# A decoder block on one core: the mLSTM norm taken for two heads at a time, its heads finished later, and the projection behind it begun later

## The chip, the cores and the metric

The program runs on one core of one Trainium2 chip. The metric is the device time of one execution in microseconds (us), from the first to the last instruction with what lies around it; lower is better. Five engines work from instruction streams of their own: TensorE (PE, with its weight loads as PEld), VectorE (DVE), ScalarE (ACT), GpSimd (POOL) and SyncE (SP), which here only issues transfers. Each stream is worked off in its order; an instruction that waits for a semaphore holds up all that stand behind it in the same stream.

## The reference, cut to what matters

One layer of a decoder with 2048 tokens of width 1024: a combined input projection, eight attention heads and four mLSTM heads side by side, an output projection over both, cross-attention to a small memory, a mixture of experts, and a final norm. The change lies in the mLSTM heads, at the step that turns numerators into normed, gated outputs:

```
num = einsum('bhcls,bhcse->bhcle', s, v) + inter_w * einsum('bhcld,bhcde->bhcle', q, C_prev)
den = sum(s) + inter_w * einsum('bhcld,bhcd->bhcl', q, n_prev)
h   = num / maximum(abs(den), exp(-m_t))
hn  = h * rsqrt(mean(h*h) + EPS)                      # per token and head
y_m = sigmoid(mo) * (hn * g_mhn + skip_m * c)
y   = concatenate([y_att, y_m]) @ w_out
```

Since the norm follows the division, the kernel never divides: it takes `num * rsqrt(mean(num*num) + EPS * max(|den|, exp(-m_t))^2)`.

## The kernel before, in words

The kernel goes through four stages: input projection, heads, cross-attention, experts. Only the heads stage is touched. There three generators are interleaved by priorities:

- `attention` works off eight attention heads, one after the other. Each multiplies scores (tiles sA, sB, L438 and L439), adds a mask and takes the row extreme on DVE (L446), exponentiates on ACT (L447), transposes (tA, tB), splits into a high and a low part on ACT and DVE (L452, L453) and multiplies with the values (oA, oB).
- `mlstm` has 16 steps: for each of four blocks of 512 tokens (`c4`) the four mLSTM heads (`h`). One step loads its tiles over SP's queue (qT, kT, nb, iwb, v), prepares nb and iwb on POOL (L748, L749), multiplies into `po`, carries the state C through DVE (L779) and copies numerators with their denominators into `num` (L781). Behind the copy `finish` of the step before is written: POOL squares num into `sq` (L712), DVE works on small tiles `sm` of 128x4 (L713 to L717, with L716 the sum of squares, and the ten instructions of the helper `rsqrt`, L28 to L32), POOL scales num into `sq` (L719), PE transposes (`ph`, L722), DVE adds the skip part (L723), POOL gates (L724) and SP stores `ym` (L725). Its inputs c2 and mo are loaded at the end of the step.
- `out_m` is the mLSTM part of the output projection, in two halves of the output rows. Each half has 16 steps of 24 matmuls into `pm` (L825 to L827), on columns of `ym` that `mlstm` has stored. POOL and ACT split `ym` first (tiles yml, ymh).

`heads` gives each generator's next step a priority that lies at a fraction of an attention head: mLSTM step i at `MEND * i / 16` heads, a step of the first half of `out_m` between `OSTART` and `OMID`, the second half between `OMID` and `OEND`. A scheduler then writes out one fixed order for each engine. A loop over `done` makes sure that the mLSTM steps that a projection step reads are placed ahead of it.

Of the kernel before, what the change touches and what calls it, by code (L numbers as in the profile page):

```python
# [8 lines left out]
F32 = mybir.dt.float32  # L9
# [3 lines left out]
OP = mybir.AluOpType  # L13
PSUM = bass.MemoryType.PSUM
DRAM = bass.MemoryType.DRAM
P = 128
# [353 lines left out]
def attention(tc, ctx, I, Z, K, marks):  # L370
# [101 lines left out]
    for pair in range(4):  # L472
# [99 lines left out]

        rb = sp.tile([32, 2, P], F32, name=f"rowB{pair}", tag="rowA", bufs=1)
        nc.vector.tensor_copy(rb, by_rows(f"stB{pair}", st[1]))
        w = op.tile([32, 2, P], F32, name=f"w{pair}", tag="w", bufs=1)

        nc.vector.tensor_sub(w[:, 0], rb[:, 0], ra[:, 0])
        nc.vector.tensor_sub(w[:, 1], ra[:, 0], rb[:, 0])
# [110 lines left out]
def mlstm(tc, ctx, I, Z, K, pb):  # L689

    nc = tc.nc

    lp = pool(tc, ctx, "p3l", 2)
    hp = pool(tc, ctx, "p3h", 2)
    cp = pool(tc, ctx, "p3c", 1)

    def const(name, shape):
        t = cp.tile(shape, F32, name="c_" + name)
        nc.sync.dma_start(t, I[name])
        return t  # L700

    yield
    ident, maskM = K["ident"], const("maskM", [P, P])
    decb, colt = K["decb"], K["colt"]
    gh = const("g_mhn", [P, 4])
    nc.vector.tensor_scalar(gh, gh, 0.5, None, op0=OP.mult)

    def finish(h, u, q0, num, c2, mo, hs, ts):

        sq = hp.tile([P, 4, P], F32, name="sq" + u, tag="sq", bufs=1)  # L710
        sm = hp.tile([P, 4, 4], F32, name="sm" + u, tag="sm", bufs=2)
        nc.gpsimd.tensor_mul(sq, num[:, :, 0:P], num[:, :, 0:P])  # L712
        nc.vector.scalar_tensor_tensor(sm[:, 1], num[:, :, 128], -1.0, num[:, :, 128], op0=OP.mult, op1=OP.max)  # L713
        nc.vector.tensor_tensor(sm[:, 1], sm[:, 1], colt[:, 2, q0:q0 + 4], op=OP.max)
        nc.vector.scalar_tensor_tensor(sm[:, 1], sm[:, 1], EPS, sm[:, 1], op0=OP.mult, op1=OP.mult)
        nc.vector.tensor_reduce(sm[:, 0], sq, axis=mybir.AxisListType.X, op=OP.add)  # L716
        nc.vector.scalar_tensor_tensor(sm[:, 0], sm[:, 0], 1.0 / P, sm[:, 1], op0=OP.mult, op1=OP.add)  # L717
        rsqrt(nc, sm[:, 3], sm[:, 0], sm[:, 1])
        nc.gpsimd.tensor_tensor(sq, num[:, :, 0:P], sm[:, 3].unsqueeze(2).to_broadcast([P, 4, P]), op=OP.mult)  # L719
        ph = pb.tile([P, 4, P], F32, name="ph" + u, tag="b")  # L720
        for i in range(4):
            nc.tensor.transpose(ph[:, i], sq[:, i], ident)  # L722
        nc.vector.scalar_tensor_tensor(c2, ph.rearrange("p i l -> p (i l)"), gh[:, h:h + 1], c2, op0=OP.mult, op1=OP.add)  # L723
        nc.gpsimd.tensor_mul(mo, mo, c2)  # L724
        nc.sync.dma_start(Z["ym"][hs, ts], mo)  # L725

    tail = None
    state = [None] * 4
    for c4 in range(4):
        for h in range(4):  # L730
            if c4 or h:
                yield
            C = state[h]
            u = f"{h}_{c4}"
            hs, ts, q0 = slice(h * P, h * P + P), slice(c4 * 512, c4 * 512 + 512), h * 16 + c4 * 4

            def load(name, src, pool=lp, bufs=2):
                t = pool.tile([P, 512], F32, name=name + u, tag=name, bufs=bufs)
                nc.sync.dma_start(t, src)
                return t  # L740

            qT, kT = (load("qk"[x] + "T", Z["mqk"][x, hs, ts]) for x in range(2))
            nb, iwb = (load(n, Z["gr"][x, q0:q0 + 4, :].rearrange("c l -> (c l)").unsqueeze(0).to_broadcast([P, 512])) for x, n in enumerate(("nb", "iwb")))
            v = lp.tile([P, 4, 129], F32, name="v" + u, tag="v")
            nc.vector.memset(v[:, :, 128:129], 1.0)
            nc.sync.dma_start(v[:, :, 0:P], Z["mv"][ts, h * P:(h + 1) * P].rearrange("(c p) e -> p c e", p=P))
            nb = nb.rearrange("p (c l) -> p c l", l=P)
            nc.gpsimd.tensor_tensor(nb, maskM.unsqueeze(1).to_broadcast([P, 4, P]), nb, op=OP.subtract)  # L748
            nc.gpsimd.tensor_mul(iwb, qT, iwb)  # L749

            pst = pb.tile([P, 4, P], F32, name="pst" + u, tag="b")
            dw = nb
            for i in range(4):
                ws = slice(i * P, i * P + P)
                nc.tensor.matmul(pst[:, i], kT[:, ws], qT[:, ws], start=True, stop=True)
                nc.scalar.activation(dw[:, i], nb[:, i], AF.Exp, bias=colt[:, 0, q0 + i:q0 + i + 1])
            nc.vector.tensor_mul(dw, pst, dw)
            pk = pb.tile([P, 4, P], F32, name="pk" + u, tag="b")
            kw = kT.rearrange("p (i d) -> p i d", i=4)
            for i in range(4):  # L760
                nc.tensor.transpose(pk[:, i], kT[:, i * P:i * P + P], ident)
            nc.vector.tensor_tensor(kw, pk, colt[:, 1, q0:q0 + 4].unsqueeze(2).to_broadcast([P, 4, P]), op=OP.mult)
            num = hp.tile([P, 4, 129], F32, name="num" + u, tag="num", bufs=2)
            for i2 in range(2):
                pt = pb.tile([P, 3, 129], F32, name=f"po{u}{i2}", tag="b")
                po, pl = pt[:, 0:2], pt[:, 2]
                for x in range(2):
                    i = 2 * i2 + x
                    ws = slice(i * P, i * P + P)
                    nc.tensor.matmul(po[:, x], dw[:, i], v[:, i], start=True, stop=(C is None), skip_group_check=True)  # L770
                    if C is not None:
                        nc.tensor.matmul(po[:, x], iwb[:, ws], C, start=False, stop=True, skip_group_check=True)
                    if c4 * 4 + i < 15:
                        nc.tensor.matmul(pl, kw[:, i], v[:, i], start=True, stop=True, skip_group_check=True)
                        Cn = hp.tile([P, 129], F32, name=f"C{u}{i}", tag=f"C{h}", bufs=2)
                        if C is None:
                            nc.vector.tensor_copy(Cn, pl)
                        else:
                            nc.vector.scalar_tensor_tensor(Cn, C, decb[:, q0 + i:q0 + i + 1], pl, op0=OP.mult, op1=OP.add)  # L779
                        C = Cn  # L780
                nc.scalar.copy(num[:, 2 * i2:2 * i2 + 2], po)  # L781
            state[h] = C
            late, tail = tail, lambda h=h, u=u, q0=q0, num=num, hs=hs, ts=ts: finish(h, u, q0, num, c2, mo, hs, ts)
            if late:
                late()

            c2, mo = (load(n, Z[n][hs, ts], hp, 1) for n in ("c2", "mo"))
    tail()


def out_m(tc, ctx, I, Z, pb, half, bufs):
# [40 lines left out]
def heads(tc, I, Z, K):  # L832

    marks = []
    with ExitStack() as ctx:
# [9 lines left out]
        with ExitStack() as c2:  # L845
# [5 lines left out]
            done = 0  # L851
            for t, which, i in sorted(at):

                while which and done < min(16, i // 4 * 4 + 5):
                    go(t, m)
                    done += 1
                if which or i == done:
# [10 lines left out]
WARM = 9  # L868
NS, NT, NO, NB = 2, 2, 2, 2
NPA, NPB = 3, 2  # L870
MEND, OSTART, OMID, OEND = 5.5, 2, 7.3, 7.9


def mm3(nc, out, wh, wl, xh, xl, first, last):
# [996 lines left out]
```

## Time and profile before

| what | value |
|---|---|
| time, median of 3 runs | 2208.98 us (2201.88 to 2212.25) |
| profiled execution: its own time, its span | 2215.31 us, 2213.5 us |
| busy over the span: PE, PEld, DVE, ACT, POOL | 2041.5, 1875.2, 1373.3, 1043.4, 635.0 us |
| heads stage, 588 to 1100 us: PE, PEld, DVE, ACT, POOL busy | 441.89, 413.08, 382.78, 324.35, 225.21 of 512.00 us |
| granted TensorE clock: span, heads stage | 0.958, 0.95 of full speed |

The profiled execution lies 6 us above the median of the three runs. "Busy" is time in which an engine works on an instruction; time in which a DVE instruction is held after it has begun counts as busy too. A busy PE is a modelled figure: matmuls overlap, so their mean durations don't add up to time. The eight attention heads begin at about 589, 658, 718, 772, 838, 891, 957 and 1022 us (the first sA matmul of each), and the stage's last matmuls (`wt`) end at about 1112 us.

### The profile page before, as it was taken

The page shows a single profiled execution, that of the slowest core. Times are in us where ns is not written, and L with a number is a line of the kernel's source. Part 1 is how long each engine was busy: PE and PEld are TensorE (multiplying, and loading weights), DVE is VectorE, ACT ScalarE, POOL GpSimd, SP SyncE. Part 2 cuts the span into 40 slices and gives each one's busy share as a digit, 9 for nine tenths or more (in the row PEclk, how much of TensorE's full clock was granted, in tenths as well). Part 3 has the DMA queues.
Part 4 walks back from the last instruction along what each step waited for, and adds up shares of the span by engine and source line. Part 5 has one row for each costly group of instructions (what it writes and reads, how often), then busy time and mean ns, then how long its engine had stood idle before and what let it go on. Part 6 is the DMA issues. An engine that isn't in the chain of part 4 may idle for free. (4 is left out here: it accounts for less than half of the span.)

```text
span 2213.5 us, 36146 instructions
## 1 busy us (share of the span) xinstructions
PE 2041.5 (92%) x13247; PEld 1875.2 (85%) x13247; DVE 1373.3 (62%) x3315; ACT 1043.4 (47%) x2216; POOL 635.0 (29%) x415
## 2 busy tenths in 40 slices
PE   8999999999888888889969999858999999999996
PEld 6898988988677888879968999857999998889985
DVE  8125741255278889865688788865666565445576
ACT  5223432233266766665534545425555554444462
POOL 3541235421344454543240020142111111121003
PEclk9999999999899999999979999968999999999998
DMA  7544645342697897786552222257878786666596
GB/s 205 178 154 142 215 144 155 113 131 111 174 236 195 242 234 216 208 228 182 180 175 72 100 96 87 87 156 239 247 222 251 202 240 193 168 188 179 152 337 236
DMA packets 276244, 402.45 MB, mean 182 GB/s; under 512 B 28176, under 2 KB 204624, under 8 KB 276016
## 3 DMA queue, kind: packets, MB, share of 16 engines
q1 hardware_dynamic: 262528, 355.11, 52.3%
q0 software_dynamic: 13536, 45.00, 8.3%
q8 instruction: 106, 1.74, 0.3%
q14 instruction: 74, 0.61, 0.1%
HBM read 286.33 MB, written 114.00 MB: 181 GB/s over the span
## 5 line engine op out<-in xcount | busy, mean ns | idle before, releaser
L39 POOL TENSOR_TENSOR wl<-wr,wh 128x1024 fp32r<-128x1024 f32 (+1 forms) x46 | 118.9, 2606 | 256.0 <-ACT wh L38 244.0
L1654 POOL DMA_INDIRECT z_acc<-y,ix x34 | 55.9, 1645 | 407.2 <-DVE y L1646 175.5
L876 PE MATMUL pa<-xl,ww_0h 128*128 128x256 f32 (+5 forms) x512 | 153.0, 307 | 2.2 <-DVE xl L42 2.2
L875 PE MATMUL pa<-xh,ww_1h 128*128 128x256 f32 (+5 forms) x512 | 152.0, 297 | 0.0
L877 PE MATMUL pa<-xh,ww_1l 128*128 128x256 f32 (+5 forms) x512 | 151.7, 296 | 0.0
L876 PE MATMUL pa<-xl,ww_1h 128*128 128x256 f32 (+5 forms) x512 | 151.6, 296 | 0.0
L877 PE MATMUL pa<-xh,ww_0l 128*128 128x256 f32 (+5 forms) x512 | 147.6, 299 | 0.0
L335 PE MATMUL pn<-wl,xh 128*128 128x256 f32 (+1 forms) x512 | 144.9, 283 | 0.0
L334 PE MATMUL pn<-wh,xh 128*128 128x256 f32 (+1 forms) x512 | 144.9, 283 | 0.0
L336 PE MATMUL pn<-wh,xl 128*128 128x256 f32 (+1 forms) x512 | 144.9, 283 | 0.0
L42 DVE SCALAR_TENSOR_TENSOR xl<-pt,f_gf,xh 128x256 fp32r<-128x256 f32 (+5 forms) x128 | 64.3, 515 | 116.5 <-ACT xh L41 116.1
L875 PE MATMUL pa<-xh,ww_0h 128*128 128x256 f32 (+5 forms) x512 | 135.4, 301 | 0.6 <-ACT xh L41 0.6
L41 ACT ACTIVATE xh<-pt,f_gf 128x256 fp32r<-128x256 f32 (+5 forms) x128 | 61.9, 499 | 135.6 <-PE pt L1576 135.2
L38 ACT CAST wh<-wr 128x1024 fp32r<-128x1024 f32 (+3 forms) x49 | 48.4, 1030 | 130.5 <-PE pn L336 58.0
L39 DVE TENSOR_TENSOR ww_1l<-ww_1r,ww_1h 128x512 fp32r<-128x512 f32 x124 | 77.6, 676 | 46.3 <-ACT ww_1h L38 46.2
L876 PEld LDWEIGHTS pa<-xl,ww_0h 128*128 128x128 f32 x512 | 97.8, 192 | 4.8 <-DVE xl L42 2.4
L877 PEld LDWEIGHTS pa<-xh,ww_0l 128*128 128x128 f32 x512 | 97.6, 192 | 0.9
L335 PEld LDWEIGHTS pn<-wl,xh 128*128 128x128 f32 x512 | 97.1, 190 | 0.9
L334 PEld LDWEIGHTS pn<-wh,xh 128*128 128x128 f32 x512 | 97.1, 190 | 0.9
L336 PEld LDWEIGHTS pn<-wh,xl 128*128 128x128 f32 x512 | 96.9, 189 | 0.5
L875 PEld LDWEIGHTS pa<-xh,ww_1h 128*128 128x128 f32 x512 | 97.4, 190 | 0.0
L877 PEld LDWEIGHTS pa<-xh,ww_1l 128*128 128x128 f32 x512 | 97.2, 190 | 0.0
(708 smaller groups left out, 7140.3 us busy)
## 6 DMA issues: line engine op xcount, KB each, us to landing
ww_1r<-w SPq DMA_DIRECT2D x31, 1024.0 KB
ww_0r<-w SPq DMA_DIRECT2D x30, 1024.0 KB
wr<-w_in SPq DMA_DIRECT2D x43, 512.0 KB
w_0r<-w SPq DMA_DIRECT2D x16, 1024.0 KB
w_1r<-w SPq DMA_DIRECT2D x16, 1024.0 KB
z_v<-v SPq DMA_DIRECT2D x32, 256.0 KB
z_mqk<-mq SPq DMA_DIRECT2D x16, 512.0 KB
kk<-z_qkh SPq DMA_DIRECT2D x32, 256.0 KB
```

The source lines that it names most:

```text
L38: a = nc.scalar.copy(hi, src)
L39: b = eng.tensor_sub(lo, src, hi.bitcast(F32))
L41: a = nc.scalar.activation(hi, src, AF.Copy, scale=scale)
L42: b = eng.scalar_tensor_tensor(lo, src, scale, hi.bitcast(F32), op0=OP.mult, op1=OP.subtract)
L334: nc.tensor.matmul(ps[:, :n], xhw, wh[:, k, :], start=(k == 0), stop=False)
L335: nc.tensor.matmul(ps[:, :n], xhw, wl[:, k, :], start=False, stop=False)
L336: nc.tensor.matmul(ps[:, :n], xlw, wh[:, k, :], start=False, stop=(k == KT - 1))
L875: nc.tensor.matmul(out, wh, xh, start=first, stop=False, skip_group_check=True)
L876: nc.tensor.matmul(out, wh, xl, start=False, stop=False, skip_group_check=True)
L877: nc.tensor.matmul(out, wl, xh, start=False, stop=last, skip_group_check=True)
L1654: d = nc.gpsimd.indirect_dma_start(out=Z["acc"], out_offset=bass.IndirectOffsetOnAxis(ap=self.ix[:r, n:n + 1], axis=0), in_=y[:r], in_offs ...
```

## The change

`finish` is cut in two. `norms` takes two heads at once, from one tile `nums` that holds the numerators of both: the squares and their sum are still formed per head, and all other small DVE instructions run once on 128x8 instead of twice on 128x4. `finish` keeps the scaling, the transposes, the gate and the store. Two heads' norms are taken in the odd step; the heads are finished one in each of the next steps, the even one in the first of them. c2 and mo are loaded (`fetch`) behind the finish of the head ahead of them. To make room, iwb has one buffer in place of two, and a small attention tile `w` shares a buffer with wtB. The loop over `done` asks for one mLSTM step more, and `OSTART` goes from 2 to 2.4.

```diff
-        w = op.tile([32, 2, P], F32, name=f"w{pair}", tag="w", bufs=1)
+        w = op.tile([P, 4, P], F32, name=f"w{pair}", tag="wtB")[0:32, 0:2]
...
-    def finish(h, u, q0, num, c2, mo, hs, ts):
-
-        sq = hp.tile([P, 4, P], F32, name="sq" + u, tag="sq", bufs=1)
-        sm = hp.tile([P, 4, 4], F32, name="sm" + u, tag="sm", bufs=2)
-        nc.gpsimd.tensor_mul(sq, num[:, :, 0:P], num[:, :, 0:P])
-        nc.vector.scalar_tensor_tensor(sm[:, 1], num[:, :, 128], -1.0, num[:, :, 128], op0=OP.mult, op1=OP.max)
-        nc.vector.tensor_tensor(sm[:, 1], sm[:, 1], colt[:, 2, q0:q0 + 4], op=OP.max)
+    def norms(c4, h, nums):
+
+        u = f"{h}_{c4}"
+        sm = hp.tile([P, 4, 2, 4], F32, name="sm" + u, tag="sm", bufs=2)
+        em = colt[:, 2, h * 16:h * 16 + 32].rearrange("p (g c) -> p g c", g=2)[:, :, c4 * 4:c4 * 4 + 4]
+        den = nums[:, :, :, 128]
+        nc.vector.scalar_tensor_tensor(sm[:, 1], den, -1.0, den, op0=OP.mult, op1=OP.max)
+        nc.vector.tensor_tensor(sm[:, 1], sm[:, 1], em, op=OP.max)
         nc.vector.scalar_tensor_tensor(sm[:, 1], sm[:, 1], EPS, sm[:, 1], op0=OP.mult, op1=OP.mult)
-        nc.vector.tensor_reduce(sm[:, 0], sq, axis=mybir.AxisListType.X, op=OP.add)
+        for g in range(2):
+            sq = hp.tile([P, 4, P], F32, name=f"sq{u}{g}", tag="sq", bufs=1)
+            nc.gpsimd.tensor_mul(sq, nums[:, g, :, 0:P], nums[:, g, :, 0:P])
+            nc.vector.tensor_reduce(sm[:, 0, g], sq, axis=mybir.AxisListType.X, op=OP.add)
         nc.vector.scalar_tensor_tensor(sm[:, 0], sm[:, 0], 1.0 / P, sm[:, 1], op0=OP.mult, op1=OP.add)
         rsqrt(nc, sm[:, 3], sm[:, 0], sm[:, 1])
-        nc.gpsimd.tensor_tensor(sq, num[:, :, 0:P], sm[:, 3].unsqueeze(2).to_broadcast([P, 4, P]), op=OP.mult)
+        return sm[:, 3]
+
+    def finish(h, u, num, rn, hs, ts):
+        c2, mo = ahead.pop()
+        sq = hp.tile([P, 4, P], F32, name="sn" + u, tag="sq", bufs=1)
+        nc.gpsimd.tensor_tensor(sq, num[:, :, 0:P], rn.unsqueeze(2).to_broadcast([P, 4, P]), op=OP.mult)
...
+    def fetch():
+
+        if tail and not ahead:
+            h, u, _, _, hs, ts = tail[0]
+            ahead.append([load(n + u, n, Z[n][hs, ts], hp, 1) for n in ("c2", "mo")])
...
-            nb, iwb = (load(n, Z["gr"][x, q0:q0 + 4, :].rearrange("c l -> (c l)").unsqueeze(0).to_broadcast([P, 512])) for x, n in enumerate(("nb", "iwb")))
+            nb, iwb = (load(n + u, n, Z["gr"][x, q0:q0 + 4, :].rearrange("c l -> (c l)").unsqueeze(0).to_broadcast([P, 512]), lp, 2 - x) for x, n in enumerate(("nb", "iwb")))
...
-            num = hp.tile([P, 4, 129], F32, name="num" + u, tag="num", bufs=2)
+            if h % 2 == 0:
+                nums = hp.tile([P, 2, 4, 129], F32, name="num" + u, tag="num", bufs=2)
+            num = nums[:, h % 2]
...
-            late, tail = tail, lambda h=h, u=u, q0=q0, num=num, hs=hs, ts=ts: finish(h, u, q0, num, c2, mo, hs, ts)
-            if late:
-                late()
-
-            c2, mo = (load(n, Z[n][hs, ts], hp, 1) for n in ("c2", "mo"))
-    tail()
+
+            if tail:
+                finish(*tail.pop(0))
+            if h % 2:
+                rn = norms(c4, h - 1, nums)
+                for g in range(2):
+                    hg = h - 1 + g
+                    tail.append((hg, f"{hg}_{c4}", nums[:, g], rn[:, g], slice(hg * P, hg * P + P), ts))
+            fetch()
+    while tail:
+        finish(*tail.pop(0))
+        fetch()
...
-                while which and done < min(16, i // 4 * 4 + 5):
+                while which and done < min(16, i // 4 * 4 + 6):
...
-MEND, OSTART, OMID, OEND = 5.5, 2, 7.3, 7.9
+MEND, OSTART, OMID, OEND = 5.5, 2.4, 7.3, 7.9
```

What the scheduler makes of it is seen in the order of each engine's instructions. On DVE before, in the second attention head (the `sm` tiles of mLSTM heads 0 and 1 of block 1), the small `sm` instructions of two heads run through each other, between the attention's mask instructions (L446, shown as ISA) and splits (L453):

```order
L713 SCALAR_TENSOR_TENSOR sm_1_9284<-num_1_9115 128x4
L446 ISA pB_20_5643,stB_4867<-sB_20_5638,b_maskB 128x128
L446 ISA stB_4867 128x1
L32 SCALAR_TENSOR_TENSOR sm_1_9141<-sm_1_9141 128x4
L453 TENSOR_TENSOR ptbl_4863<-tB_0_3_5563,ptbh_4862 128x512
L714 TENSOR_TENSOR sm_1_9284<-sm_1_9284,colt 128x4
L30 SCALAR_TENSOR_TENSOR sm_1_9141<-sm_1_9141 128x4
L446 ISA pB_21_5646,stB_4867<-sB_20_5638,b_maskB 128x256
L446 ISA stB_4867 128x1
L715 SCALAR_TENSOR_TENSOR sm_1_9284<-sm_1_9284 128x4
L31 TENSOR_TENSOR sm_1_9141<-sm_1_9141 128x4
L32 SCALAR_TENSOR_TENSOR sm_1_9141<-sm_1_9141 128x4
```

On DVE after, where the third attention head begins, the same two mLSTM heads have one chain (128x8), with other instructions between its links as before:

```order
L32 SCALAR_TENSOR_TENSOR sm_1_9107<-sm_1_9107 128x8
L797 SCALAR_TENSOR_TENSOR C_11_9171<-C_10_9166,decb,po_10_9162 128x129
L453 TENSOR_TENSOR ptbl_4865<-tB_3_3_5728,ptbh_4864 128x512
L30 SCALAR_TENSOR_TENSOR sm_1_9107<-sm_1_9107 128x8
L446 ISA pA_3_5854,stA_5805<-sA_2_5846,b_maskA 128x256
L446 ISA stA_5805 128x1
L582 TENSOR_TENSOR rowX_5525<-w_5753,rowX_5525 32x128
L583 TENSOR_TENSOR rowB_5748<-w_5753,rowB_5748 32x128
L446 ISA pA_4_5869,stA_5805<-sA_4_5864,b_maskA 128x256
L446 ISA stA_5805 128x1
L31 TENSOR_TENSOR sm_1_9107<-sm_1_9107 128x8
```

DVE's stream has 2906 rows after and 3020 before. On SP's queue in the first attention head before, the loads of mLSTM step 1 (its iwb here) and step 2 stood ahead of the loads of the values vA and vB:

```order
L325 DMA z_mo<-g_3_4788 128x1024
L739 DMA iwb_0_8755<-z_gr 128x512
L746 DMA v_0_8757<-z_mv 128x4x128
L405 DMA kk_5298<-z_qkh 64x1024 x2
L739 DMA qT_0_8833<-z_mqk 128x512
L402 DMA qs_5297<-z_qkh 64x1024
L403 DMA qs_5297<-z_qkl 64x1024
L405 DMA kk_5298<-z_qkh 64x1024 x2
L483 DMA vA_4870<-z_v 32x16x128 x4
L485 DMA vB_4871<-z_v 128x4x128 x4
```

On SP's queue after, iwb of step 1 stands behind them, since its single buffer is free only when step 0 has used it:

```order
L405 DMA kk_5298<-z_qkh 64x1024 x2
L828 DMA womr_9202<-w_out 128x512
L483 DMA vA_4870<-z_v 32x16x128 x4
L485 DMA vB_4871<-z_v 128x4x128 x4
L738 DMA iwb_0_8751<-z_gr 128x512
L738 DMA kT_0_8824<-z_mqk 128x512
L738 DMA nb_0_8826<-z_gr 128x512
L762 DMA v_0_8830<-z_mv 128x4x128
```

In the same way every later iwb moved behind the last use of the one ahead of it. On POOL after, at the end of the second attention head, the scalings of the two heads of a pair (sn) stand one behind the other, and the second waits for the transposes of the first, since both use one buffer:

```order
L39 TENSOR_TENSOR yml_9225<-yml_9225,ymh_9224 128x1024
L462 TENSOR_TENSOR numB_4869<-numB_4869,fB_3_5744 64x512
L728 TENSOR_TENSOR sn_1_9186<-num_1_9005,sm_1_9107 128x512
L728 TENSOR_TENSOR sn_1_9311<-num_1_9005,sm_1_9107 128x512
L765 TENSOR_TENSOR iwb_1_9264<-qT_1_9258,iwb_1_9264 128x512
L764 TENSOR_TENSOR nb_2_9379<-c_maskM,nb_2_9379 128x512
```

Before, each scaling had stood apart from the next, with its head's squares ahead of it. On PE, the rows between the starts of the attention heads show what moved there: of the 768 `pm` matmuls of the stage, 264 stood ahead of the seventh head's first score before and 216 do now; 462 stood ahead of the eighth's and 402 do now.

## Rows read from the trace of the kernel before

**Rows 1.** Busy time of each engine by attention head, then heads 0 to 5 together

```profile
core 0: us, PE busy (x) PEld busy (x) DVE busy (x) ACT busy (x) POOL busy (x), PEclk, DMA share, GB/s
588.80:657.70 68.90, 51.13 (x312) 46.15 (x313) 43.67 (x148) 38.67 (x115) 29.28 (x23) 0.85 0.97 257
657.70:717.70 60.00, 51.33 (x349) 46.26 (x347) 49.13 (x163) 42.30 (x121) 26.20 (x21) 0.97 0.81 200
...
891.00:959.00 68.00, 57.79 (x378) 53.01 (x378) 56.13 (x158) 43.62 (x118) 39.48 (x31) 0.92 0.76 202
959.00:1020.00 61.00, 53.44 (x377) 51.37 (x376) 33.34 (x101) 35.75 (x93) 29.70 (x20) 0.92 0.73 208
1020.00:1070.00 50.00, 49.50 (x390) 48.74 (x390) 31.31 (x88) 30.78 (x83) 9.79 (x5) 1.00 0.60 179
...
588.00:960.00 372.00, 313.74 (x2125) 288.82 (x2125) 300.91 (x930) 244.99 (x688) 180.83 (x141) 0.94 0.86 227
```

**Rows 2.** The sm instructions alone, 588 to 960 us, summed

```profile
core 0: us, DVE busy (x) POOL busy (x), PEclk, DMA share, GB/s
588.00:960.00 372.00, 90.70 (x240) 16.66 (x16) 0.94 0.86 227
```

**Rows 3.** The sm instructions by line: min/median/max in ns

```profile
L30 DVE SCALAR_TENSOR_TENSOR sm<-sm x48: 141/159/1186, 618.3 to 949.5; 128x4 f32<-128x4 f32 x48
L714 DVE TENSOR_TENSOR sm<-sm,colt x16: 145/164/2202, 616.5 to 940.8; 128x4 f32<-128x4 f32 x16
L716 DVE TENSOR_REDUCE sm<-sq x16: 667/679/687, 616.9 to 941.9; 128x4 f32<-128x512 f32 x16
```

**Rows 4.** DVE in order of time: start us, duration us, instruction

```profile
850.56 1.46 DVE L586 TENSOR_TENSOR w<-w,rowX 32x256 f32<-32x256 f32 x1
851.95 0.99 DVE L713 SCALAR_TENSOR_TENSOR sm<-num 128x4 f32<-128x4 f32 x1
852.98 1.20 DVE L714 TENSOR_TENSOR sm<-sm,colt 128x4 f32<-128x4 f32 x1
854.10 0.68 DVE L828 TENSOR_TENSOR xm<-pm,xm 128x512 f32<-128x512 f32 x1
854.70 0.15 DVE L715 SCALAR_TENSOR_TENSOR sm<-sm 128x4 f32<-128x4 f32 x1
```

**Rows 5.** POOL in order of time over the same stretch

```profile
850.46 1.29 POOL L748 TENSOR_TENSOR nb<-c_maskM,nb 128x512 f32<-128x512 f32 x1
851.71 1.22 POOL L712 TENSOR_TENSOR sq<-num 128x512 f32<-128x512 f32 x1
852.89 1.26 POOL L749 TENSOR_TENSOR iwb<-qT,iwb 128x512 f32<-128x512 f32 x1
```

**Rows 6.** What PE waited for, 588 to 960 us: total us, times, longest

```profile
PE pst L755 <- DMA kT<-z_mqk: 6.0, 1, 6.0
PE ph L722 <- POOL sq L719: 6.0, 4, 2.6
PE oA L511 <- ACT ptah L452: 5.5, 5, 3.5
PE oA L511 <- DMA vA<-z_v: 5.1, 1, 5.1
PE sA L438 <- DVE stA L446: 4.4, 4, 1.8
...
PE tB L552 <- DVE ptbl L453: 0.2, 1, 0.2
```

**Rows 7.** iwb on SP's queue, then on POOL: start us, duration us

```profile
602.02 0.32 SPq L739 DMA_DIRECT2D iwb<-z_gr  x1
609.75 1.27 POOL L749 TENSOR_TENSOR iwb<-qT,iwb 128x512 f32<-128x512 f32 x1 [2.23 <-DMA iwb<-z_gr]
665.09 0.42 SPq L739 DMA_DIRECT2D iwb<-z_gr  x1
672.60 1.27 POOL L749 TENSOR_TENSOR iwb<-qT,iwb 128x512 f32<-128x512 f32 x1 [0.17 <-DMA iwb<-z_gr]
```

**Rows 8.** What POOL waited for, 588 to 960 us: total us, times, longest

```profile
POOL nb L748 <- DMA nb<-z_gr: 34.2, 10, 8.0
POOL sq L719 <- DVE sm L32: 30.1, 10, 8.5
...
POOL sq L712 <- PE ph L722: 8.4, 1, 8.4
POOL iwb L749 <- DMA iwb<-z_gr: 3.5, 3, 2.2
```

More of the change, by code (lines that the diff above doesn't have):

```diff
@@ L725, in finish, with load @@
         nc.sync.dma_start(Z["ym"][hs, ts], mo)
-    tail = None
+    def load(name, tag, src, pool=lp, bufs=2):
+        t = pool.tile([P, 512], F32, name=name, tag=tag, bufs=bufs)
+        nc.sync.dma_start(t, src)
+        return t
+    tail, ahead = [], []
+    def fetch():
+        if tail and not ahead:
+            h, u, _, _, hs, ts = tail[0]
+            ahead.append([load(n + u, n, Z[n][hs, ts], hp, 1) for n in ("c2", "mo")])
     state = [None] * 4
@@ L735, in mlstm @@
             hs, ts, q0 = slice(h * P, h * P + P), slice(c4 * 512, c4 * 512 + 512), h * 16 + c4 * 4
[L737 to L742, printed above, removed]
-            nb, iwb = (load(n, Z["gr"][x, q0:q0 + 4, :].rearrange("c l -> (c l)").unsqueeze(0).to_broadcast([P, 512])) for x, n in enumerate(("nb", "iwb")))
+            qT, kT = (load("qk"[x] + "T" + u, "qk"[x] + "T", Z["mqk"][x, hs, ts]) for x in range(2))
+            nb, iwb = (load(n + u, n, Z["gr"][x, q0:q0 + 4, :].rearrange("c l -> (c l)").unsqueeze(0).to_broadcast([P, 512]), lp, 2 - x) for x, n in enumerate(("nb", "iwb")))
             v = lp.tile([P, 4, 129], F32, name="v" + u, tag="v")
```

## The prediction, made before the changed kernel ran

> **What bounds the kernel now.** I first read the busy time by attention head [rows 1], since the change lies in the heads stage alone. In heads 0 to 5 (588 to 960 us), where the mLSTM steps run, no engine is full: PE is busy 313.74 of 372 us, DVE 300.91, ACT 244.99, POOL 180.83. PE and DVE are both near their limit and wait for each other. In head 7 (1020 to 1070 us) there is no mLSTM work left, and PE is busy 49.50 of 50 us: there PE is the bound. The first head has another limit, transfers: DMA is at 0.97 there, PE at 51.13 of 68.90 us.
>
> Next I read what PE waited for in heads 0 to 5 [rows 6]. The 26 rows of that answer sum to 57.1 us; 11.1 us of it is two transfers in head 0. Of the other 46.0 us, 28.2 us ended with a DVE instruction, 11.8 with an ACT instruction and 6.0 with POOL's scaling, which itself had waited 30.1 us in ten places for the last link of DVE's norm chain [rows 8]. So DVE's backlog is what a shorter norm can relieve, and 46 us is all that there is to win in PE's waits.
>
> Then the norm itself. The `sm` instructions of the 16 heads take 90.70 us of DVE, 240 instructions [rows 2]. The 16 sums of squares (L716) are steady, 667 to 687 ns [rows 3], 10.9 us together. That leaves 79.8 us for 224 small ones, 0.356 us each, though a median one takes 0.16 us: some take 1.2 to 2.2 us [rows 3]. The two timelines show why. L713 starts at 851.95 and ends at 852.94 us, where POOL's L712 ends (852.93); L714 ends at 854.18, where POOL's L749 ends (854.15); L715, with POOL idle, takes 0.15 us [rows 4, 5]. A small DVE instruction on SBUF tiles that meets a POOL instruction is held until that one ends, and all DVE work behind it is held too. L828, which reads PSUM and one SBUF tile, takes its usual 0.68 us.
>
> **The change, part by part.**
>
> *Fewer small DVE instructions.* Per pair of heads 2 x 14 small ones become 14, on twice the elements; the sums of squares stay. That is 112 fewer over eight pairs. I price each at 0.356 us, holds included, since POOL's work stays as it was (16 squares, 16 scalings, 16 gates) and the remaining ones meet it as often: 112 x 0.356 = 39.9 us less DVE time. The lower bound per instruction is the median 0.16 us, 17.9 us in all. [...]
>
> How much of 39.9 us reaches the end? DVE is idle 71 of 372 us in these heads, so not all of its work is waited for. If PE's 46.0 us of waits shrank only as DVE's work does (39.9 of 300.9, 13%), the gain would be 6 us. If DVE were the bound throughout, it would be 39.9 us. I take half of the upper one, 20 us, because DVE and PE are within 13 us of the same load.
>
> *Heads finished one to two steps later.* POOL's scaling no longer stands right behind the chain it needs; the 6.0 us that PE waited for it can go, which I count inside the 20 us. On the other side the second scaling of a pair waits for the transposes of the first, one buffer being shared, with iwb and nb behind it on POOL. Before, a square that waited for transposes cost POOL 8.4 us, once [rows 8]; POOL is busy only half the time. I take +1 us, bounds 0 and 8.
>
> *iwb with one buffer.* Its load can now be issued only when the last step has made its last use, and POOL's product must follow before PE goes on. From issue to POOL's start took 7.7 us (602.02 to 609.75) and 7.5 us (665.09 to 672.60), with POOL waiting at the end; the product takes 1.27 us [rows 7]: some 9 us. Heads 0 to 5 hold 1855 PE rows of the order in 368 us, 0.20 us a row. Between the last use of one iwb and the first of the next the new order puts 37 to 105 rows; ten of the 15 gaps have 54 or more (10.8 us and up) and hide the 9 us, five have 37 to 50 (7.4 to 10 us) and may fall short by up to 2 us each. Step 1 is one of these five, and its load stands behind eight value loads of 256 KB, which at that head's 257 GB/s [rows 1] take 8 us; it can fall short by 5 more. I take +3 us, upper bound 15. What would stand behind a late iwb is PE's own stream, attention's matmuls too, and POOL's adds.
>
> *Projection later.* By the order, 60 `pm` matmuls move from ahead of head 7 to behind its start. At that head's pace (49.50 us for 390 matmuls, 0.127 us each [rows 1]) this is 7.6 us more in a stretch where nothing hides it. It is paid back only if PE's work was what set the earlier heads' length. As PE and DVE share that, I take half, +4 us; bounds 0 and 7.6.
>
> *The rest.* `w` in wtB's buffer and c2, mo loaded behind the finish ahead: no cost, as `w` is used between two pairs' wtB tiles, and a head's gate now comes a step after its norm. Without that cover, one load of about 7.5 us per late head would be waited for on POOL.
>
> Sum: -20 + 1 + 3 + 4 = -12 us. The profiled execution (2215.31 us) would become 2203 us. It lies 6 us above the median of 2208.98; off the median the forecast is **2197 us**, 0.54% faster. A measurement of this kernel tells about 0.5%, 11 us, from no change.
>
> **The rivals.**
>
> 1. *DVE was the bound of heads 0 to 5.* Then all 39.9 us return, less about 5 for iwb and the moved matmuls: some 2174 us. For it: DVE is busy 49.13 of 60.00 us in head 1 and 56.13 of 68.00 in head 5 [rows 1], and its holds stop the attention's mask instructions in the same stream. Against it: PE is at 51.33 and 57.79 in the same heads, so the next limit is close.
>
> 2. *Only the unheld part is saved.* If a hold moves on to the next DVE instruction with SBUF tiles (L586 was held to 1.46 us as well [rows 4]), 112 instructions free 17.9 us; half of it reaches the end, 9 us, and the 8 us of costs eat it: 2208 us, the same. [...]
>
> 3. *The single iwb buffer decides, slower.* If a load takes 9 to 11 us instead of 7.5, with DMA at 0.76 to 0.97 in these heads [rows 1], the five short gaps miss by 2 to 4 us and step 1 by 5 or more, some 20 us of PE waits in all, with the 7.6 us of moved projection unpaid: 20 + 8 + 1 - 9 (DVE's relief halved, since PE then waits for transfers) = +20, about 2229 us. It decides from a mean landing of about 10 us on. For it: nb, loaded just as late today, is what POOL waits longest for, 34.2 us [rows 8]. Against: POOL waited for iwb only 3.5 us in three places [rows 8], and most gaps have room.
>
> **How the numbers follow.** My forecast (a gain of 5 to 20 us) has 0.45, rival 1 0.16, rival 2 0.22, rival 3 0.17. Faster by over 0.5%: rival 1 and about three quarters of the forecast, 0.50. Slower by over 0.5%: most of rival 3 and a little of rival 2's tail, 0.18. The same: 0.32. The range runs from rival 1's time to a rival 3 of half its size: 2172 to 2220 us. The forecast's own range is 2189 to 2204 us.
>
> **What would show it right or wrong.** Right: 112 small `sm` instructions instead of 224, at some 0.36 us, and DVE busy near 261 us in heads 0 to 5; the eighth attention head starting some 15 to 20 us earlier than at 1022 us, and the time from there to the stage's end longer by up to 8 us; PE's waits on DVE down from 28.2 to about 15 us. For rival 1: the eighth head over 30 us earlier. For rival 2: DVE's busy time down by less than 20 us, with L586 or L582 to L584 held for longer. For rival 3: PE's L790 or POOL's L765 waiting for iwb's transfer for over 15 us in total. The prediction is wrong if PE's waits in heads 0 to 5 don't shrink while DVE's work does: then DVE was not what they came from.

## The result, and the profile after

The changed kernel is slower: 2223.60 us against 2209.53 us (medians of 12 runs each), ratio 1.0065 with a 95% interval of 1.0049 to 1.0082, 14 us where 12 us of gain were forecast. The profiled execution took 2222.09 us (span 2220.3), 6.8 us more than that of the kernel before (2215.31), which lay above its median. So what the two traces show against each other covers about half of the loss.

Busy time in heads 2, 5 and 7 of the changed kernel and in heads 0 to 5 together, in the columns of [rows 1] (its head 7 begins 1.6 us into the window given for it):

```profile
712.70:774.80 62.10, 50.99 (x338) 48.79 (x339) 42.94 (x135) 36.09 (x103) 32.70 (x26) 0.89 0.91 232
...
898.70:957.30 58.60, 48.52 (x305) 43.25 (x303) 39.10 (x132) 38.23 (x107) 28.67 (x24) 0.94 0.78 188
...
1022.00:1070.00 48.00, 48.00 (x386) 47.63 (x386) 30.62 (x84) 30.09 (x77) 11.37 (x6) 1.00 0.56 166
588.00:960.00 372.00, 309.84 (x2064) 288.38 (x2063) 260.56 (x810) 240.28 (x682) 172.03 (x135) 0.91 0.85 217
```

The `sm` instructions alone, as in [rows 2], and then by line, as in [rows 3]:

```profile
588.00:960.00 372.00, 45.53 (x128) 16.63 (x16) 0.91 0.85 217
```

```profile
L30 DVE SCALAR_TENSOR_TENSOR sm<-sm x24: 90/162/1940, 645.9 to 953.6; 128x8 f32<-128x8 f32 x24
L720 DVE TENSOR_REDUCE sm<-sq x16: 616/684/690, 614.8 to 946.3; 128x4 f32<-128x512 f32 x16
```

DVE did what was forecast of it: 260.56 us in place of 300.91, 40.3 less. The 112 small instructions that remain take (45.53 - 16 x 0.684) / 112 = 0.31 us each; on twice the elements their median is nearly unchanged (159 and 162 ns for L30) and they are still held, up to 1.94 us in that line: the one of 1.94 us ends at 868.78 us, where POOL's L39 ends (868.76). The `sm` instructions alone fell by 45.2 us; the rest of DVE's work in the window takes 4.8 us more.

But the heads are no shorter. The first, seventh and eighth attention head begin at 587.0, 957.2 and 1023.6 us (588.8, 957.3 and 1022.4 before): the first six take 370.2 us in place of 368.5. The `wt` matmuls end the stage, before and then after (shortest, median and longest in ns, then first and last start in us):

```profile
L604 PE MATMUL wt<-w,sel x64: 416/416/577, 1097.3 to 1111.7; 32*128 32x128 f32 x64
```

```profile
L604 PE MATMUL wt<-w,sel x64: 416/416/577, 1105.3 to 1119.9; 32*128 32x128 f32 x64
```

From the eighth head's start to the first of them it takes 81.7 us in place of 74.9, and 7 to 8 us stay to the end (last `px` at 1463.7 against 1455.5, last `pa` at 2160.8 against 2153.9).

What PE waited for, 588 to 960 us (total us, times, longest), beside [rows 6]:

```profile
PE tA L493 <- ACT pA L447: 12.3, 3, 6.4
PE oA L511 <- DMA vA<-z_v: 7.8, 1, 7.8
PE pst L771 <- DMA kT<-z_mqk: 6.9, 1, 6.9
PE sA L438 <- DVE stA L446: 6.0, 7, 2.7
PE po L790 <- POOL iwb L765: 5.6, 4, 2.4
```

By releaser all rows of this answer sum to: DVE 20.9 us (28.2 before), ACT 19.3 (11.8), POOL 6.4 (6.0), transfers 14.7 (11.1); in all 61.3 against 57.1. DVE's share fell by 7.3 us, ACT's rose by 7.5. The largest row was 1.6 us, once, before: waits for an exponential on ACT. What ACT did at the longest (start us, us, instruction, idle time ahead of it and its releaser), and the load it stood behind, on SP's queue:

```profile
722.73 0.59 ACT L452 CAST ptah<-tA 128x512 fp32r<-128x512 f32 x1
730.33 1.04 ACT L38 CAST ymh<-yml 128x1024 fp32r<-128x1024 f32 x1 [7.01 <-DMA yml<-z_ym]
731.28 0.50 ACT L447 ACTIVATE pA<-pA,stA 128x256 f32<-128x256 f32 x1
```

```profile
719.69 0.43 SPq L837 DMA_DIRECT2D yml<-z_ym  x1
```

The exponential that PE needs stands behind L38, the cast of the projection's input, and L38 stands for a load that was issued at 719.69 and landed 10.6 us later. PE stands from 725.55 to 731.93 us, and DVE for nearly as long. What ACT waited for such loads in heads 0 to 5 (total us, times, longest), before and then after:

```profile
ACT ymh L38 <- DMA yml<-z_ym: 12.6, 4, 3.7
```

```profile
ACT ymh L38 <- DMA yml<-z_ym: 19.9, 5, 7.0
```

The exponential that starts at 731.28 us had its input from DVE's L446 by 723.3 us: it stood for 8 us, 7.01 of them with ACT idle ahead of L38.

PE lost time twice here: it stood for 6.4 us, and then it ran at a granted clock of 0.50. The same columns as above, in steps of 4 us around it:

```profile
724.00:728.00 4.00, 1.55 (x14) 1.36 (x13) 2.72 (x13) 0.00 (x0) 0.00 (x0) 1.00 1.09 238
728.00:732.00 4.00, 0.07 (x1) 0.07 (x2) 0.00 (x0) 1.67 (x4) 0.50 (x1) 0.85 1.06 220
732.00:736.00 4.00, 4.00 (x18) 3.71 (x19) 2.60 (x9) 3.92 (x13) 3.13 (x2) 0.50 1.16 195
...
740.00:744.00 4.00, 4.00 (x37) 4.00 (x37) 2.50 (x8) 2.37 (x8) 3.45 (x3) 1.00 0.47 149
```

From 732 to 736 us, after the wait, the granted clock is 0.50, and a full PE starts 18 matmuls in these 4 us where it starts 37, of another mix, at 1.00 from 740 to 744. In the four stretches of 60 us from 650 us on the clock was 0.97, 0.97, 1.00 and 0.97 before and is 0.91, 0.90, 0.90 and 0.97 now.

How much of PE's work left heads 0 to 5 is seen in the `pm` matmuls alone, before and then after (busy time of PE, PEld, DVE and ACT, then clock, DMA share and GB/s):

```profile
588.00:960.00 372.00, 37.19 (x266) 34.00 (x267) 7.50 (x11) 0.00 (x0) 0.94 0.86 227
```

```profile
588.00:960.00 372.00, 30.80 (x225) 28.54 (x226) 6.18 (x9) 0.00 (x0) 0.91 0.85 217
```

There are 61 matmuls fewer (2064 against 2125), and 41 of them are `pm`; of the other 20, eight (sA) now stand ahead of the window, since the first head begins at 587.0 us. At the 0.127 us of [rows 1] they are 7.7 us of PE's work. PE's busy time fell by 3.9 us only, so the rest runs 3.8 us slower; PE's idle time rose by the same 3.9 us (62.2 of 372 against 58.3). In a window of fixed length these figures must add up, so they name no cause. They say that PE had less to do and got no further: slower matmuls and new waits took what the moved work had freed. At the eighth head's start 60 `pm` matmuls are missing (402 against 462), and they come on top in the last head.

### The profile page after: what moved, and what is told of

It is laid out like the page before. It is cut to its first block, busy times and chain, and to the rows that moved or that the text cites. A ratio compares the mean times of both kernels' runs of the same rounds, so it can differ in the third digit from the quotient of the medians.

```text
span 2220.3 us, 36051 instructions
## 1 busy us (share of the span) xinstructions
PE 2040.6 (92%) x13247; PEld 1877.5 (85%) x13247; DVE 1338.7 (60%) x3203; ACT 1043.0 (47%) x2216; POOL 631.3 (28%) x415
## 5 line engine op out<-in xcount | busy, mean ns | idle before, releaser
L39 POOL TENSOR_TENSOR wl<-wr,wh 128x1024 fp32r<-128x1024 f32 (+1 forms) x46 | 118.9, 2606 | 256.0 <-ACT wh L38 221.1
L38 ACT CAST wh<-wr 128x1024 fp32r<-128x1024 f32 (+3 forms) x49 | 48.4, 1030 | 132.5 <-PE pn L336 58.0
L39 DVE TENSOR_TENSOR ww_1l<-ww_1r,ww_1h 128x512 fp32r<-128x512 f32 x124 | 77.7, 676 | 45.9 <-ACT ww_1h L38 45.8
L900 PEld LDWEIGHTS pa<-xl,ww_1h 128*128 128x128 f32 x512 | 98.0, 191 | 0.0
```

Of the source, the lines that this page charges most:

```text
L38: a = nc.scalar.copy(hi, src)
L39: b = eng.tensor_sub(lo, src, hi.bitcast(F32))
L900: nc.tensor.matmul(out, wh, xl, start=False, stop=False, skip_group_check=True)
```

## The experiments

Each ratio is to the kernel before, run on the same chip, with its 95% interval; 0.001 is 2.2 us.

**DVE's relief alone, two ways.** e1 takes 96 small DVE instructions out of the kernel before, two of the three refinements in the helper `rsqrt`, and edits nothing else. The scheduler writes a new order of every engine for it, as for each kernel below: of the 3157 matmuls of the stage that both traces hold, at most 1577 keep the order that they had among each other. So each run tests its edit together with a new order.

```diff
-        rsqrt(nc, sm[:, 3], sm[:, 0], sm[:, 1])
+        rsqrt(nc, sm[:, 3], sm[:, 0], sm[:, 1], 1)
```

> The kernel before, with one refinement of the inverse square root in the norm in place of three: 96 small DVE instructions fewer, and nothing else edited (a less exact norm). At 0.356 us each this is 34 us less DVE time in heads 0 to 5. If DVE paced these heads (my prediction's step), the time falls by 10 to 20 us, to about 2195. If DVE's work there is not what PE waits for, as the changed kernel suggests (DVE 40 us less busy, heads 0 to 5 as long as before), it stays within 5 us of before.

Measured: 0.9994 (0.9978 to 1.0009). DVE is busy 271.1 us in heads 0 to 5, 30 us less, and nothing comes back. PE's waits there, the first rows:

```profile
PE tA L493 <- ACT pA L447: 17.7, 6, 4.2
PE sA L438 <- DVE stA L446: 6.3, 7, 3.2
```

Its waits on DVE fell from 28.2 to 19.2 us, those on ACT rose from 11.8 to 25.8. ACT stood longer for the projection's input:

```profile
ACT ymh L38 <- DMA yml<-z_ym: 21.4, 8, 4.6
```

e8 keeps the norm by pairs, the heads finished later, `w` in wtB's buffer and the step more in the loop over `done`, and undoes the rest (a `num` tile per head in three buffers, two iwb buffers, `OSTART` 2):

> The control with two iwb buffers and the projection begun at 2 heads again: the norm by pairs alone is left. If heads 0 to 5 have a pace of their own that neither DVE nor the projection sets, it has the time of the kernel before within 5 us. If the shorter norm does help once iwb is early, it is faster than before by 5 to 15 us.

Measured: 1.0006 (0.9992 to 1.0020), with DVE at 271.2 us. Two reliefs of DVE by 30 us, made in different ways, are worth nothing. In e8 too PE's waits on DVE fell (23.6 us) and those on ACT rose (22.1), but ACT stood for another load, that of nb, which POOL's product waits for (before: 10.4 us for nb, 12.6 for the projection's input):

```profile
ACT nb L773 <- POOL nb L765: 24.5, 10, 6.4
...
ACT ymh L38 <- DMA yml<-z_ym: 6.2, 5, 3.3
```

**One iwb buffer, and the later projection, in the kernel before.** e2 gives iwb one buffer, e3 sets `OSTART` to 2.4.

> The kernel before with one buffer for iwb, and nothing else edited. If the late load of iwb is what ate the DVE time saved, this alone makes the kernel slower by 10 to 20 us (about 2225). If iwb is hidden, or only costs the 5.6 us that PE waited for POOL's iwb product in the changed kernel, it is slower by 0 to 6 us.

> The kernel before with the projection begun at 2.4 heads in place of 2, and nothing else edited. If the loss is the projection's matmuls that move to the last head (60 of them, 0.127 us each), and heads 0 to 5 don't get shorter for them, it is slower by 6 to 10 us (about 2217). If PE's own work paced heads 0 to 5, it is the same.

Measured: e2 1.0047 (1.0029 to 1.0065), some 10 us; e3 1.0013 (0.9999 to 1.0027), some 3 us, which can't be told from nothing. What POOL waited for in e2, beside [rows 8]:

```profile
POOL nb L748 <- DMA nb<-z_gr: 45.9, 10, 10.2
...
POOL iwb L749 <- DMA iwb<-z_gr: 10.5, 4, 6.5
```

iwb is late by 10.5 us in place of 3.5, PE's waits on POOL rise from 6.0 to 14.6 us, and nb, loaded over the same queue, is later too (45.9 us of POOL's waits in place of 34.2).

**The parts in the changed kernel.** e4 undoes the later projection alone (`OSTART` 2). e5 is the changed kernel with a `num` tile per head, which leaves room for the next two: e6 adds the second iwb buffer, e7 a buffer of its own for the scaled numerators.

> The changed kernel with the projection begun at 2 heads again. If the moved projection is the loss, the time comes back by 8 to 14 us, to about 2210 to 2215. If the loss is in iwb or in the pairs' finish, it stays at 2220 or more.

> The changed kernel with one numerator tile per head in three buffers in place of the shared tile of two heads; the first small instruction then runs once per head (8 more in all). It makes room for a second iwb buffer, and is the control for the two kernels that use it. Each theory expects the changed kernel's time within 5 us, about 2223 where the kernel before has 2209.

> The control with two iwb buffers again. If the single iwb buffer is the loss, it is faster than the control by about 10 us, that is at the time of the kernel before or up to 5 us above. If the pairs' finish or the longer way to a head's end is the loss, it stays at the control's time.

> The control with a buffer of its own for the scaled numerators, so that squares no longer wait for the transposes of the scaled ones (22.1 us of POOL waits in the changed kernel). If this POOL wait is part of the loss, it is faster than the control by 3 to 8 us. If POOL's wait is idle time that costs nothing, within 3 us.

Measured: e4 1.0092 (1.0073 to 1.0111), e5 1.0050 (1.0030 to 1.0069), e6 1.0037 (1.0021 to 1.0053), e7 1.0054 (1.0035 to 1.0074). So the shared buffer of squares and scaled numerators costs nothing that can be seen (e7 beside e5). One iwb buffer costs 3 us with the later projection (e5 beside e6, their intervals overlap) and 19 us with the early one (e4 beside e8, which differ in the `num` tiles and in the chip too). The later projection costs 7 us with two iwb buffers (e6 beside e8); with one it gives back 6 us (the changed kernel beside e4, their intervals overlap). And with one iwb buffer the pairs are no longer free: e4 lies 10 us above e2, which has that buffer and the early projection without the pairs. The parts don't add: each variant is a new order with other waits.

**What paces the heads: transfers, or PE.** e9 and e11 leave out 8.4 MB of loads each, e9 those of nb, which lands late, and of iwb, e11 others (c2 and mo). e10 is e8 with the edit of e9. e12 takes PE work out.

```diff
-            nb, iwb = (load(n, Z["gr"][x, q0:q0 + 4, :]...) for x, n in enumerate(("nb", "iwb")))
+            nb, iwb = (lp.tile([P, 512], F32, name=n + u, tag=n, bufs=2) for n in ("nb", "iwb"))
...
+                    if half:
                         nc.tensor.matmul(ps[:, i], wl[:, ws], yh[:, k], start=False, stop=(k == 3))
```

> The kernel before with the loads of nb and iwb left out: POOL's two products read one constant tile of 32 columns instead, so the weights of the mLSTM are wrong and 32 loads of 256 KB, 8.4 MB, are gone from heads 0 to 5; the work of the four engines stays. It asks what paces these heads. If it is the transfers' rate (84 MB in 372 us, 227 GB/s), 8.4 MB less is up to 37 us: heads 0 to 5 end 20 to 37 us earlier and the kernel takes about 2175 to 2190 us. If it is the late landing of nb (POOL waited 34.2 us for it), 10 to 30 us come back here too, and e11, with as many bytes less, shows that it was not the rate. If the engines pace each other (PE at 314 of 372 us with its waits on DVE and ACT), the time stays within 10 us of before.

> The kernel of e8 (norm by pairs, two iwb buffers, projection from 2: the relief of DVE alone) with the same constant in place of nb and iwb as in e9, so the weights are wrong here too. Set against e9 it says what 40 us less DVE work are worth once these loads are gone. If transfers had hidden DVE's relief, this is 5 to 20 us faster than e9. If DVE is not on the path that sets the heads' length at all, it equals e9 within 6 us, as e8 equals before.

> The kernel before with the loads of c2 and mo left out, the last gate reading a constant instead, so the mLSTM's output is wrong: as many bytes less as in e9 (8.4 MB), but nb and iwb still land as late as before. If the rate of the transfers paces heads 0 to 5, this gains as much as e9 (20 to 37 us). If the late landing of nb does, it gains little (under 8 us) where e9 gains. If the engines do, neither gains.

> The kernel before with one of the three matmul passes of the first half of the output projection left out (a less exact product): 128 matmuls of 256 columns fewer in heads 2 to 7, at 0.127 us each 16 us less PE work. If PE's own work paces these heads, 10 to 16 us come back, also in heads 2 to 5; if transfers pace heads 0 to 5, only the share that lies in head 6 and 7 comes back, about 4 to 6 us; if nothing of PE is on the path, nothing.

Measured: e9 0.9953 (0.9940 to 0.9966), e10 1.0013 (0.9996 to 1.0029), e11 0.9990 (0.9975 to 1.0005), e12 0.9982 (0.9965 to 0.9999). The rate of the transfers is not the limit: 8.4 MB fewer gain nothing (e11). That the same bytes gain 10 us where they are nb's and iwb's (e9) speaks for lateness. PE's own work is no plain bound either: 16 us less of it is worth 4 us, hardly more than nothing by the interval. e10 fitted neither theory: with the pairs e9's gain is gone. In heads 0 to 5 e10 is no worse than e9 (2179 matmuls against 2168, PE's waits 52.1 us against 56.1); it falls behind afterwards, with 375 matmuls against 448 from 960 to 1020 us. Why is not settled.

**The late load of the projection's input.** e13 and e14 leave that load out of the changed kernel and of the kernel before, for seven of the first half's eight chunks. e15 and e16 do the same to e9 and e10, so that neither of the two late loads is left.

```diff
-        nc.sync.dma_start(raw, Z["ym"][:, ts].rearrange("(k p) t -> p k t", p=P))
+        if half or not c:
+            nc.sync.dma_start(raw, Z["ym"][:, ts].rearrange("(k p) t -> p k t", p=P))
```

> The changed kernel with the loads of the projection's input left out in its first half, but for the first chunk (seven loads of 512 KB; each later chunk splits again what is left in the tile, so the output is wrong): ScalarE's cast L38 can't be late for a transfer there. If ScalarE standing behind that load is where DVE's relief went (19.9 us of waits in heads 0 to 5, against 12.6 before), the time falls by 10 to 18 us against the changed kernel, to or below the kernel before (ratio 0.997 to 1.002). If another wait steps in, as after every change so far, it stays within 5 us of the changed kernel (ratio 1.004 to 1.009).

> The same loads left out of the kernel before (the output is wrong here too). By the first theory the gain is smaller than in e13, 4 to 10 us (ratio 0.995 to 0.998), as ScalarE waited 12.6 us there and not 19.9. By the other it is within 5 us of before.

> The kernel of e9 (constant in place of nb and iwb) with the projection's loads left out as in e14. If the late loads are what DVE's relief was hidden behind, this lies 10 to 20 us below before (ratio 0.991 to 0.995). It is the base for e16.

> The kernel of e10 (norm by pairs, constant in place of nb and iwb) with the projection's loads left out as in e14. Set against e15: if DVE's 40 us were hidden behind late loads alone, this is now 5 to 20 us faster than e15. If DVE isn't what the heads wait for, with or without late loads, it equals e15 within 5 us or is slower, as e10 was slower than e9 by 13 us.

Measured: e13 1.0631 (1.0598 to 1.0665), e14 1.0613 (1.0577 to 1.0649), e15 0.9889 (0.9854 to 0.9924), e16 0.9882 (0.9845 to 0.9918). The first two totals can't be read against the kernel before: the last `pa` matmul is followed by 194 us of work where it is 59 in the changed kernel, with matmuls into a tile `pav` that the kernels of the comparison don't run; the experts' load depends on the data. The first `wt` matmul starts 11.5 us earlier in e13 than in the changed kernel (1093.8 against 1105.3) and 7.5 us earlier in e14 than before (1089.8 against 1097.3), as the first theory has it. But that is one execution each: e13's took 5 us less than its median and the one of before 6 us more than its own, so neither difference is clear of the scatter.

Against each other the two totals can be read, since both have the 194 us behind the last `pa`. The medians of five runs are 2348.85 us (e13) and 2347.60 (e14); the means are 2.4 us apart, with a 95% interval of -4 to 9 worked out from the ten times. With the loads the same two kernels are 14 us apart (11 to 18). So without these loads most of the changed kernel's loss is gone, by whatever wait it came. It isn't PE's waits on ACT in heads 0 to 5 that went, 18.9 us in place of 19.3, since ACT now stands for nb (10.2 before this edit); the 6.9 us are the first chunk's load, which e13 keeps:

```profile
ACT nb L772 <- POOL nb L764: 20.3, 9, 8.0
...
ACT ymh L38 <- DMA yml<-z_ym: 6.9, 1, 6.9
```

With both late loads gone (e15) the kernel before is 26 us faster at the medians, more than the 10 to 20 us expected. Its first `wt` matmul starts 24 us earlier (1073.2 against 1097.3), so the gain lies in the heads. Heads 0 to 5 of e15, then of e16, in the columns of [rows 1]:

```profile
588.00:960.00 372.00, 325.00 (x2261) 305.00 (x2261) 312.55 (x964) 259.40 (x720) 188.50 (x145) 0.94 0.80 212
```

```profile
588.00:960.00 372.00, 329.39 (x2301) 310.24 (x2300) 288.64 (x877) 263.42 (x739) 193.23 (x148) 0.94 0.79 214
```

In the same 372 us PE gets through 2261 matmuls in place of 2125 (its waits on ACT are 6.7 us in place of 11.8), and with the pairs through 2301. e16 lies below e15 by 3.8 us at the medians (2182.90 and 2186.72 us, four runs each), and the intervals overlap: once these loads are gone DVE's relief may be worth some 4 us, which these runs can't tell from nothing. (The two traces are further apart, 2179.29 and 2190.24 us: the fastest of e16's four runs and the slowest of e15's.)

**Only the order of that cast.** e17 and e18 keep all loads and work, and have the scheduler put ACT's cast behind the last `num` copy of the newest mLSTM step:

```diff
-        split(nc, yh, yl, raw, nc.gpsimd)
+        with ExitStack() as order:
+            if Z["behind"] and not half:
+                order.enter_context(tc.issue_after(Z["behind"].ins))
+            split(nc, yh, yl, raw, nc.gpsimd)
```

> The changed kernel with one rule more for the scheduler: ScalarE's cast of the projection's input (ymh, L38) stands behind the last num copy of the newest mLSTM step, which puts it 8, 20, 20, 13 and 9 rows later in ScalarE's order for the first five chunks (some 3 to 7 us at 0.36 us a row, 240 us in 682 instructions); loads and results stay. If ScalarE standing behind that load is where DVE's relief went, its wait in heads 0 to 5 falls from 19.9 us to under 8, PE's long waits behind it go, and the time falls by 6 to 14 us, to about the kernel before (ratio 0.999 to 1.004). If the wait only moves on to nb or elsewhere, the ratio stays at 1.005 to 1.009.

> The same rule in the kernel before, where ScalarE waited 12.6 us for that load in heads 0 to 5; the cast stands 12 to 19 rows later for the first three chunks. By the first theory 3 to 8 us are gained (ratio 0.996 to 0.9985), and this is the fastest version that still computes everything. By the other the ratio is 0.999 to 1.003.

Measured: e17 1.0028 (1.0007 to 1.0049), e18 1.0027 (1.0015 to 1.0039). What ACT waited for in e17, the two rows that bear on this:

```profile
ACT nb L772 <- POOL nb L764: 21.7, 10, 7.7
...
ACT ymh L38 <- DMA yml<-z_ym: 2.5, 1, 2.5
```

In e17 the wait falls from 19.9 to 2.5 us, PE's waits on ACT from 19.3 to 12.3, and 8 us of the 14 are back (the interval meets that of the changed kernel at 1.0049). But ACT stands longer for nb (21.7 us against 10.2), and PE's waits on POOL rise from 6.4 to 10.0. Nor does the trace show the gain: this execution took 2222.54 us, as long as the changed kernel's (2222.09). The gain lies in the medians. e18 is a miss: the cast's wait is gone there too, and the kernel is 6 us slower. Heads 0 to 5 of e18:

```profile
588.00:960.00 372.00, 317.22 (x2118) 294.83 (x2119) 296.44 (x917) 240.97 (x680) 180.61 (x141) 0.92 0.84 225
```

PE's waits are 53.7 us in place of 57.1, but the granted clock is 0.92 in place of 0.94, and PE is busy 3.5 us longer on seven matmuls fewer. After 960 us PE waits 7.5 us for the cast that now comes later; before it was 4.8. None of the versions that compute everything is faster than the kernel before.

## Why the prediction was wrong

**The step that failed** is the one that turned DVE time into kernel time: "I take half of the upper one, 20 us, because DVE and PE are within 13 us of the same load." The 39.9 us themselves were right (40.3), and so was the price of an instruction, holds included (0.36 us forecast, 0.31 measured on twice the elements). What they were worth at the end is 0 by e1 and e8, in the setting of the kernel before; with one iwb buffer the pairs even cost 10 us (e4 beside e2). That two engines are near the same load doesn't say that either sets the time: PE's waits of [rows 6] were put down to DVE, and when DVE came earlier PE waited for the next thing, in the longest case an exponential on ACT that stood behind a late load. PE's waits on DVE fell to 20.9 us, not to about 15. The text named the sign of this itself: PE's waits not shrinking while DVE's work does. They went from 57.1 to 61.3 us.

**iwb's single buffer** was mis-sized. It was put at +3 us with 15 as the upper bound; it measures 10 us in the kernel before (e2), and with the pairs 3 or 19 us by where the projection stands. The price of the load was not what failed: where POOL waited for iwb's transfer in the changed kernel, it was 5.4 to 7.4 us from issue to POOL's start, no more than the 7.5 us of the sum. What moved is the issue. Step 1's iwb was issued at 602.02 us [rows 7] and is now at:

```profile
621.55 1.10 SPq L738 DMA_DIRECT2D iwb<-z_gr  x1
```

POOL's waits for iwb's transfer were 3.5 us before, 8.7 after, 10.5 in e2 and 21.8 in e4. So the gaps, counted in rows of the order, hid less than the sum took them to.

**The moved projection** behaved as written where it was looked at: the stretch behind the eighth head's start is 6.8 us longer, with 7.6 us forecast. It was put at +4 net; it measures +3 (e3), +7 (with two iwb buffers) and, with one, a gain of 6 us. The last sign was not forecast; it isn't clear of the noise.

**Heads finished later** was put at +1 us for the shared buffer, which costs nothing that can be seen (e7), though POOL's squares now wait 22.1 us for transposes in place of 8.4. PE's 6.0 us of waits for the scaling went, as the text said they could (0.8 us are left), without a gain at the end. Finishing later was not run without the pairs.

**The sum, in its measured parts**: pairs and later finish +1 us (e8), one iwb buffer behind them +19 (e4), later projection -6, in all +14. As steps from one kernel to the next they must add up to the whole. By another path the terms differ: one iwb buffer alone +10 (e2), the pairs on it +10 (e4), later projection -6.

**The rivals.** Rival 1 (DVE the bound) is excluded by e1. Rival 2 (only the unheld part is saved) falls too, since all 40.3 us were saved; its time, the same as before, is what the pairs alone give, for another reason. Rival 3 had the direction: its own sign, over 15 us of waits for iwb at L790 or L765, came to 5.6 + 8.7 = 14.3 us. Its condition, a mean landing of about 10 us, did not come about (5.4 to 7.4 us where POOL waited), so that its time lay near is in part luck. What it lacked is that DVE's relief would be worth nothing at all and that waits for a second load, the projection's, would grow as well.

**Shown and not shown.** Shown: DVE's relief is worth nothing beside the kernel before, in two new orders (e1, e8); the rate of the transfers isn't the limit (e11); taking both late loads away gives 26 us (e15); without the loads of the projection's input the changed kernel's loss is mostly gone (e13 beside e14). Supported: that it loses the time where ACT stands for that load. Putting the cast later gives 8 of 14 us back (e17), but the interval meets that of the changed kernel, and in e13 PE's waits on ACT stay. Nor do ACT's waits for this load go with the time: they are 21.4 us in e1 and 6.2 in e8, and both kernels are as fast as before with 12.6. Not shown: that this wait bounds the kernel before; e18 speaks against it. What a new order costs without any other edit was not run, and e18, which moves one cast, lost 6 us. Why e9's gain goes with the pairs (e10) is open, and a second buffer for yml was not tried.

## What to carry to other kernels

When engines wait for each other in fixed orders, the releaser that a profile names can be the last of several that were nearly as late: before pricing a relief, ask what releases the same instruction next, and test it by shortening the suspect alone (as e1 does, though under a new order) instead of taking a share of its busy time. Look for instructions that wait for a load in the stream of a busy engine, since what is ready can stand behind them (here an exponential that had its input by 723.3 us and started at 731.28), and look at the granted clock behind a long wait of PE as well (here 0.50 from 732 to 736 us, behind 6.4 us of waiting; that the wait brought it about was not tested). An edit that frees room by giving up a second buffer should be measured in the kernel that will hold it: the same buffer was worth 3 (within the noise), 10 and 19 us here.

## What was not expected of the hardware

After PE's wait of 6.4 us its granted clock stood at 0.50 from 732 to 736 us (18 matmuls started, against 37 at 1.00). PE's waits of heads 0 to 5 grew by 4 us only, from 57.1 to 61.3, but with longer ones among them (behind head 0 the longest was 3.5 us and is 6.4), and the clock of these heads went from 0.94 to 0.91. Whether the longer waits are the reason was not tested. The loads of 512 KB that ACT stood for in heads 0 to 5 took 4.7 to 9.8 us from issue to use in the kernel before and 5.3 to 10.6 us in the changed one, at a high DMA share whether they were short or long: 0.97 at 313 GB/s from 738 to 744 us before, where one took 5.7 us, and 1.05 at 215 GB/s from 719.7 to 730.3 us after, where one took 10.6. And 8.4 MB fewer transfers in a stretch with a DMA share of 0.86 moved the time by less than 0.3%.
